# Hybrid encoder trunk, last FFN: second product by Strassen's scheme, with sums of weights made by accumulating DMAs

## The chip, the cores and the metric

The kernel runs on one core of one Trainium2 chip. The time is that of one execution on the device in microseconds (us); lower is better. Where several runs are named, their median is meant. TensorE is PE (its weight loads PEld), VectorE DVE, ScalarE ACT, GpSimd POOL, SyncE SP.

## The reference, cut to what matters

A trunk of two layers on 512 tokens of width 1024. Each layer has a token mixer and then a SwiGLU FFN, each of them between two RMS norms, with shift, scale and gate from a conditioning vector. The change touches the second layer's FFN, the last thing computed, and its tail:

```python
def swiglu_ffn(h, w_in, w_out):
    gate, up = jnp.split(h @ w_in, 2, axis=-1)
    return (jax.nn.silu(gate) * up) @ w_out        # (512 x 2816) @ (2816 x 1024)

def reference(...):
    ...
        h = rmsnorm(x, norm_g[i, 2]) * (1.0 + scale) + shift
        y = swiglu_ffn(h, f_w_in[i], f_w_out[i])
        x = x + gate * rmsnorm(y, norm_g[i, 3])
    return x
```

Everything is float32. The kernel makes a float32 product on TensorE from two parts of each operand: a high part, rounded to the format `fp32r`, and a low part, the difference from it. Three matmuls stand for one: high x high, high x low, low x high.

## The kernel before

The last FFN is the call `ffn(3, 1, ...)` at the kernel's end. Its first product (`w1`, 1024 x 5632) gives gate and up, 22 blocks of 128 rows each, with tokens along the free dimension (512 in one PSUM bank). The first six blocks (`lead_ps`) are begun in the boundary behind the mixer and finished by `rest`; the other 38 are made by `in_chunk`, 24 matmuls of 128x512 each. `load_w` (L209 to L222) loads two blocks of weights (1 MB) over SP's queue into a `wst` buffer and has `split_w` (L203, L204) make the two parts in a `whl` buffer: ACT casts the high part, DVE subtracts. For each f, `ff_act` (L964 to L968) takes silu of the gate on ACT, multiplies by up on DVE, casts the high part on ACT and subtracts on DVE. So the 22 activation tiles `ff0` to `ff21` (128 rows of the hidden dimension x 512 tokens, two parts) lie ready before the second product.

The second product is made by `out_begin`, `out_finish` and `Boundary` (L346 on). For each column half of `w2` (512 columns) and each k of 22, `mm_tiles` (L378 to L380) multiplies the four token groups of 128 by the two parts of the weights: 22 x 4 x 2 x 3 matmuls. Token groups are output rows here, and the eight results (two halves, four groups) fill all eight PSUM banks. Weights of 4 x 128 rows x 512 columns come by `load_wo` (L233) into `wst` buffers and are split into `whl` tiles of two row blocks. At the end each token group in turn gets its last matmuls (`m0`, `m1a`, `m1b`), the sum of squares on ACT (`sq`, L427), the product with the gate and norm row on DVE (`yg_`, L431), the root (`rt1`, L441), the reciprocal (`rc1`, L444) and the new x (`x`, L448), which SP's queue stores; the last half of the last group is cut in two (`x_end`, L456 and L457).

Buffers: `wst` has 2, `whl` 4, `t2` (temporaries of 128x512) 4; the eight `h` tiles hold the FFN's input. The order of PE, ACT and DVE is written out by hand in the boundaries and at the end (`manual_schedule`), and in the first layer's FFN; in this `ffn` a scheduler sets it, except for PE in `rest`. Instructions of an engine run in order, and so do the DMAs of a queue: one that waits holds up what is behind it.

Of the kernel before, what the change touches and what calls it, by code (L numbers as in the profile page):

```python
# [8 lines left out]
F32 = mybir.dt.float32  # L9
F32R = mybir.dt.float32r  # L10
AF = mybir.ActivationFunctionType
# [5 lines left out]
P = 128  # L17
T = 512
D = 1024
KD = D // P  # L20
DFF = 2816
NF = DFF // P
# [13 lines left out]
def trunk_kernel(  # L36
# [26 lines left out]
    def t2(name):  # L63
        return tmp.tile([P, T], F32, tag="t2", name=name, bufs=4)
# [52 lines left out]
    xt = [hp.tile([P, D], F32, name=f"x{t}", tag=f"x{t}") for t in range(4)]  # L117
# [88 lines left out]
    def load_w(srcs, nk=KD, k0=0, later=None):  # L206


        st = wst_p.tile([P, 8, 256], F32, tag="wst", name="wst")  # L209
        o = 0  # L210
        for m, c0, n in srcs:
            dma(st[:, :nk, o:o + n], m[k0 * P:(k0 + nk) * P, c0:c0 + n].rearrange("(k p) f -> p k f", p=P))
            o += n
        res = []
        for b in range(o // P):
            w = whl_p.tile([P, 2, 8, P], F32R, tag="whl", name="whl")
            sw = st[:, :nk, b * P:(b + 1) * P]
            if later is None:
                split_w(sw, w, nk)
            else:  # L220
                later.append((lambda sw=sw, w=w: act.copy(w[:, 0, :nk, :], sw),  # L221
                              lambda sw=sw, w=w: dve.tensor_tensor(w[:, 1, :nk, :], sw,  # L222
                                                                   w[:, 0, :nk, :].bitcast(F32), SUB)))
            res.append(w)
        return res
# [63 lines left out]
    def in_chunk(w, h):  # L289
        pst = mm_ps("ip")  # L290
        mm_chunk(pst, w, h)
        return pst
# [9 lines left out]
    def small(n):  # L302
        return tmp.tile([P, n], F32, tag=f"ss{n}", name="ss", bufs=8)

    gate_d = dram.tile([4, KD, P], F32, name="gate_d")
# [11 lines left out]
    def make_gg(s, gg):  # L317

        gg = gg()
        dma(gg, gate_d[s].rearrange("j p -> (j p)").partition_broadcast(P))  # L320
        return gg
# [232 lines left out]
    def out_finish(parts, *ready):  # L554
        first, second, finish = parts
        for part in (first, second):
            for ops in part:
                for op in ops:
                    op()
        return finish(*ready)  # L560
# [9 lines left out]
    with ExitStack() as ph:  # L570
# [10 lines left out]
        def act_tile(name):  # L581
            return actp.tile([P, 2, T], F32R, tag="a", name=name)
# [12 lines left out]
        h = [hp.tile([P, 2, T], F32R, tag=f"h{j}", name=f"h{j}") for j in range(4)]  # L595
# [20 lines left out]
        lead = {}  # L616
# [66 lines left out]
        with tc.manual_schedule(engines={PE_ENGINE, mybir.EngineType.SP, mybir.EngineType.Activation,  # L683
# [41 lines left out]
            s2, b1 = small(2), small(1)  # L725
# [18 lines left out]
            lead_ps = [None] * 6  # L744
# [101 lines left out]
            splits, ws, acts, us, ggs = [], [], [], {}, []  # L846
            t0 = {}

            def load_pair(p):
                jp, kind = 2 + p // 3 * 2, (1, 2, 0)[p % 3]  # L850
                ws.extend(load_w([(w_in0, kind * D + jp * P, 256)], later=splits))
# [31 lines left out]
            for p in range(2):  # L883
# [12 lines left out]
            tiles = []  # L896
            parts = out_begin(0, w_out0, lambda k: acts[k], KD, ggs, xn_tile, "aux", None,
                              ffn_after(0), ada_tile)
            for k in range(18):
                i, jp = k % 6, 2 + k // 6 * 2  # L900
# [45 lines left out]
            lead, todo = ffn_lead(0, tile4), [[] for _ in range(5)]  # L946
# [7 lines left out]
            begun = out_finish(parts, tail, ws0)  # L954


        def ffn(s, i, begun, act_tile, gg_tile, xn_tile, lead, after):
            w1, w2 = f_w_in[i], f_w_out[i]
            acts = []
            h, lead_ps, rest, more = begun  # L960

            def ff_act(psg, psu, f):
                g = t2("g")
                act.activation(g, psg, AF.Silu)  # L964
                dve.tensor_mul(g, psu, g)
                a = act_tile(f"ff{f}")
                act.copy(a[:, 0, :], g)
                dve.tensor_tensor(a[:, 1, :], g, a[:, 0, :].bitcast(F32), SUB)  # L968
                acts.append(a)

            for f in range(0, NF, 2):
                if f == 0:
                    with tc.manual_schedule(engines={PE_ENGINE}):
                        for i in (0, 2, 1, 3, 4, 5):
                            rest(i)
                    pss = lead_ps[:4]
                elif f == 2:
                    pss = lead_ps[4:] + [in_chunk(w, h) for w in more]
                else:
                    pss = [in_chunk(w, h) for w in load_w([(w1, f * P, 256)]) + load_w([(w1, DFF + f * P, 256)])]  # L980
                for b in range(2):
                    ff_act(pss[b], pss[2 + b], f + b)
                if f == 18:
                    gg = make_gg(s, gg_tile)
            return out_finish(out_begin(s, w2, lambda k: acts[k], NF, [gg], xn_tile, "aux", lead, after))

        def ssd_lead():
            return (load_lead([(wm_in, 6144, NH), (wm_in, DIN, P)], tile4)
                    + load_lead([(wm_in, DIN + P, P), (wm_in, 2 * DIN, P)], tile4)
# [3 lines left out]
        h, lead_ps, rest, more = begun  # L993
        acts, ws, splits, gates, lows, todo, ggs = [], list(more), [(), ()], {}, [], [], []
# [4 lines left out]
        def gate(f, pst):  # L999
            gates[f] = t2("g")  # L1000
            act.activation(gates[f], pst, AF.Silu)

        def up(f, pst):
            g, a = gates[f], act_tile(f"ff{f}")
            dve.tensor_mul(g, pst, g)
            act.copy(a[:, 0, :], g)
            acts.append(a)
            lows.append(lambda: dve.tensor_tensor(a[:, 1, :], g, a[:, 0, :].bitcast(F32), SUB))
# [20 lines left out]
        with tc.manual_schedule(engines={PE_ENGINE, mybir.EngineType.SP, mybir.EngineType.Activation,  # L1029
# [14 lines left out]
            tiles = []  # L1044
            for k in range(2 * NF - 6):
# [8 lines left out]
                q, j = divmod(k - 3, 4)  # L1054
# [19 lines left out]
        begun = out_finish(parts)  # L1074
        h, lead_ps, rest, wz1 = begun
# [4 lines left out]
    with ExitStack() as ph:  # L1080
# [99 lines left out]
        class Group:  # L1180
# [169 lines left out]
            def root(self):  # L1350
                self.rg = t2("rg")
                act.activation(self.rg, self.ssg, AF.Sqrt, bias=eps_t, scale=1.0 / 256)
# [201 lines left out]
        with tc.manual_schedule(engines={PE_ENGINE}):  # L1554
# [3 lines left out]
            gg2.append(make_gg(2, lambda: tile4b([P, D], F32, "gg")))  # L1558
            begun = out_finish(parts)

    with ExitStack() as ph:
        actp3 = ph.enter_context(tc.tile_pool(name="actp3", bufs=22, reuse_waits="tile"))
        ffn(3, 1, begun, lambda n: actp3.tile([P, 2, T], F32R, tag="a", name=n),
            lambda: actp3.tile([P, D], F32, tag="gg", name="gg", bufs=1), None, None, None)


# [27 lines left out]
```

## Time and profile before

| | |
|---|---|
| median of 3 runs | 1366.4 us (1366.18 to 1366.81) |
| the profiled execution: its time | 1366.3 us |
| its span (first to last instruction in the trace) | 1364.5 us |
| last FFN, first product by `in_chunk` | 1031.8 to 1238.5 us |
| last FFN, second product | 1238.5 to 1358.4 us |
| from the last matmul to the end of the span | 1358.5 to 1364.5 us |
| mean granted clock of TensorE | 0.999 |

All times inside the profile count from the start of the span. A row of a group names the line, the engine, the operation, the tiles (output <- inputs), their shapes and the count; behind the bar the busy time in us and the mean of one in ns, then the idle time of the engine just ahead of them and what ended it. In a timeline or a chain the first number is the start in us, the second the length. The busy time of one instruction overlaps that of the next by a little, so the step from one start to the next is shorter than the length of one.

### The profile page before, as it was taken

What the parts mean: (1) busy time and instruction counts of PE and PEld (TensorE: products, weight loads), DVE (VectorE), ACT (ScalarE), POOL (GpSimd) and SP (SyncE); (2) the same over time, 40 slices, a digit from 0 to 9 for tenths busy, and PEclk for the clock granted to TensorE, in tenths of its full rate; (3) what the DMA queues carried; (4) which work ended last, traced back from release to release, by engine and by line L of the source; (5) the groups of instructions that cost most, each with busy time, mean ns of one, the idle gap of its engine ahead of it and who ended that gap; (6) DMA issues with size and microseconds to landing.
All of it is one profiled execution on the core that took longest, in us unless ns stands there. A gap on an engine that the chain in (4) does not pass through costs nothing.

```text
span 1364.5 us, 17280 instructions
## 1 busy us (share of the span) xinstructions
PE 1353.1 (99%) x6975; PEld 1139.0 (83%) x6975; DVE 849.5 (62%) x1344; ACT 539.6 (40%) x826; POOL 11.6 (1%) x23
## 2 busy tenths in 40 slices
PE   8999999999999999999999999999999999999998
PEld 6788889888888888898888888888898888888886
DVE  5578766787776322759988898897672333333224
ACT  5333355222322222745655545464572232222112
POOL 0000000000000000000000000000000000000000
PEclk9999999999999999999999999999999999999999
DMA  9767750777776232325343433313502332222221
GB/s 311 233 182 241 230 198 17 251 227 246 223 241 215 97 111 90 108 62 160 108 140 110 138 97 105 131 60 119 184 27 83 107 105 98 93 93 93 93 93 62
DMA packets 154212, 190.35 MB, mean 140 GB/s; under 512 B 5892, under 2 KB 111252, under 8 KB 153108
## 3 DMA queue, kind: packets, MB, share of 16 engines
q1 hardware_dynamic: 149984, 176.34, 40.8%
q10 hardware_dynamic: 4148, 12.90, 3.1%
q8 instruction: 55, 0.90, 0.3%
q14 instruction: 25, 0.20, 0.0%
HBM read 186.98 MB, written 2.24 MB: 139 GB/s over the span
## 4 chain that ended last, share of the span: by engine, by line
PE 97%; SPq 2%; DMA 1%; ACT 0%; DVE 0%; issue 0%; DVEq 0%; ACTq 0%
PE ip L276 18%; PE ip L278 18%; PE ip L277 18%; PE y L378 9%; PE y L380 9%; PE y L379 9%; PE li L276 3%; PE li L278 3%; PE li L277 3%; PE li L756 1%; PE yd L1313 1%; SPq L611 1%; PE yo L1307 1%; PE xtr L494 1%; DMA ada_st<-in_ada_w_dram 1%; PE cb L1252 1%
## 5 line engine op out<-in xcount | busy, mean ns | idle before, releaser
L276 PE MATMUL ip<-h,whl 128*128 128x512 f32 x1096 | 430.8, 393 | 0.2 <-DVE cv L863 0.2
L278 PE MATMUL ip<-h,whl 128*128 128x512 f32 x1096 | 426.8, 389 | 0.0
L277 PE MATMUL ip<-h,whl 128*128 128x512 f32 x1096 | 426.5, 389 | 0.0
L276 PEld LDWEIGHTS ip<-h,whl 128*128 128x128 f32 x1096 | 205.8, 188 | 43.9 <-issue 1.8
L278 PEld LDWEIGHTS ip<-h,whl 128*128 128x128 f32 x1096 | 205.7, 188 | 43.3
L277 PEld LDWEIGHTS ip<-h,whl 128*128 128x128 f32 x1096 | 205.8, 188 | 41.8
L204 DVE TENSOR_TENSOR whlo<-wsto,whlo 128x1024 fp32r<-128x1024 f32 x63 | 76.9, 1224 | 162.8 <-ACT whlo L203 162.7
L222 DVE TENSOR_TENSOR whl<-wst,whl 128x1024 fp32r<-128x1024 f32 x96 | 116.7, 1221 | 59.8 <-ACT whl L221 59.6
L378 PE MATMUL y<-whlo,ff 128*128 128x512 f32 x352 | 137.1, 390 | 0.0
L380 PE MATMUL y<-whlo,ff 128*128 128x512 f32 x352 | 136.9, 389 | 0.0
L379 PE MATMUL y<-whlo,ff 128*128 128x512 f32 x352 | 136.9, 389 | 0.0
L203 ACT CAST whlo<-wsto 128x1024 fp32r<-128x1024 f32 x63 | 65.8, 1051 | 162.6 <-PE y L380 149.5
L204 DVE TENSOR_TENSOR whl<-wst,whl 128x1024 fp32r<-128x1024 f32 (+1 forms) x77 | 72.7, 973 | 87.4 <-ACT whl L203 87.4
L124 DVE SCALAR_TENSOR_TENSOR ada_acc<-ada_st,csil,ada_acc 128x512 f32<-128x512 f32 x140 | 105.0, 750 | 4.0 <-DMA ada_st<-in_ada_w_dram 0.5
L221 ACT CAST whl<-wst 128x1024 fp32r<-128x1024 f32 x96 | 99.8, 1041 | 4.1 <-DMA wst<-in_m_w_in_dram 2.4
L203 ACT CAST whl<-wst 128x1024 fp32r<-128x1024 f32 (+1 forms) x77 | 62.6, 846 | 91.1 <-PE ip L278 39.8
L276 PE MATMUL li<-h,whl 128*128 128x256 f32 x288 | 83.2, 289 | 0.0
L278 PE MATMUL li<-h,whl 128*128 128x256 f32 x288 | 81.6, 283 | 0.0
L277 PE MATMUL li<-h,whl 128*128 128x256 f32 x288 | 81.5, 283 | 0.0
L380 PEld LDWEIGHTS y<-whlo,ff 128*128 128x128 f32 x352 | 66.1, 188 | 13.8
L379 PEld LDWEIGHTS y<-whlo,ff 128*128 128x128 f32 x352 | 66.1, 188 | 13.7
L378 PEld LDWEIGHTS y<-whlo,ff 128*128 128x128 f32 x352 | 66.1, 188 | 13.5
(235 smaller groups left out, 1643.9 us busy)
## 6 DMA issues: line engine op xcount, KB each, us to landing
ada_st<-in_ada_w_dram SPq DMA_DIRECT2D x96, 512.0 KB, 5.1
wst<-in_f_w_in_dram SPq DMA_DIRECT2D x44, 1024.0 KB, 5.2
wsto<-in_f_w_out_dram SPq DMA_DIRECT2D x20, 1024.0 KB, 5.0
wst<-in_m_w_in_dram SPq DMA_DIRECT2D x14, 1024.0 KB, 5.4
wst<-in_m_w_in_dram SPq DMA_DIRECT2D x20, 512.0 KB, 5.3
wst<-in_a_w_in_dram SPq DMA_DIRECT2D x9, 1024.0 KB, 6.0
csb<-cs_d ACTq DMA_DIRECT2D x8, 1024.0 KB, 5.1
wsto<-in_m_w_out_dram SPq DMA_DIRECT2D x7, 1024.0 KB, 6.4
```

What stands on the lines that cost most here:

```text
L124: dve.scalar_tensor_tensor(acc, w, csil[:, k:k + 1], acc, MUL, ADD)
L203: act.copy(dst[:, 0, :nk, :], src)
L204: dve.tensor_tensor(dst[:, 1, :nk, :], src, dst[:, 0, :nk, :].bitcast(F32), SUB)
L221: later.append((lambda sw=sw, w=w: act.copy(w[:, 0, :nk, :], sw), lambda sw=sw, w=w: dve.tensor_tensor(w[:, 1, :nk, :], sw, w[:, 0, :nk, : ...
L222: lambda sw=sw, w=w: dve.tensor_tensor(w[:, 1, :nk, :], sw, w[:, 0, :nk, :].bitcast(F32), SUB)))
L276: pe.matmul(dst, w_at(w, 0, kk), a[:, 0, sl], start=start, stop=False)
L277: pe.matmul(dst, w_at(w, 0, kk), a[:, 1, sl], start=False, stop=False)
L278: pe.matmul(dst, w_at(w, 1, kk), a[:, 0, sl], start=False, stop=stop)
L378: pe.matmul(pst, a[:, 0, tk], wt[:, 0, kk, :], start=k == 0, stop=False)
L379: pe.matmul(pst, a[:, 0, tk], wt[:, 1, kk, :], start=False, stop=False)
L380: pe.matmul(pst, a[:, 1, tk], wt[:, 0, kk, :], start=False, stop=k == K - 1)
L494: pe.transpose(pt[:, j * 256 + t * P:j * 256 + (t + 1) * P], self.xn[2 * hi + t][p // 2][:, c:c + P], ident)
```

## The change

The second product of the last FFN is cut 2 x 2 x 2: the 512 tokens into halves of 256, the 1024 columns into halves of 512, and the 22 row blocks of the hidden dimension into two sets of 11, the even and the odd ones. A pair of neighbouring row blocks, p = 0 to 10, gives one block to each set, so `b11`, `b12`, `b21`, `b22` of a pair are four quarters of 128 x 512 (first digit: row set, second: column half), and `a11`, `a12`, `a21`, `a22` of 128 x 256 (first digit: token half, second: row set). Strassen's scheme in Winograd's form makes seven products of halves. Products 1 to 7 are, in this order, b11 with a11; b21 with a12; b22 with a12; b22 with a11; b12 with s1; b11 with a21; b21 with a22, where every name but the first few stands for what lies in that place by then: sums of quarters.

* Sums of activations are made by DVE in place (`s13`, `a_prep`); the unsplit activations lie in `raw`, and `s1` in `s1t`.
* Sums of weights are made by DMAs from GpSimd's queue with `accum_op=ADD`: T1 (b12 += b11), T3 (b11, reloaded with the raw b12 by SP's queue, += b22), T2 (b22 += b12), T4 (b21 += b22). Units are two double pairs, (0,1) and (2,3), and seven single ones; one DMA each per unit and sum.
* The weights of the second product are loaded whole: units 0 to 2 into `w2t` tiles during the first product, 3 and 4 into `wst` buffers at its end, 5 to 8 into the `h` tiles once the first product is over.
* The 77 steps (product, p) are taken in pairs, "tiles" n = 0 to 38. For each, `w_prep(n)` makes the two parts of the weights in a `whl` buffer (4 of them) and `a_prep(n)` those of the activations in an `ao` buffer (3), ACT casting and DVE subtracting; `products` issues the matmuls, 12 for a tile. After the matmuls of tile n come `behind(n)` (sums of products out of the banks A, B, C, D, epilogue work, and the DMAs for T2 to T4), then `w_prep(n + 4)` and `a_prep(n + 3)`. The order of all engines is written by hand from the start of this FFN.
* Results: 11 = A after product 1, plus B; 12 = C - A after product 4, + D; 22 = D - A after product 6; 21 = A after product 7. The first token half is finished while products 6 and 7 run; the last three tiles are issued for token group 2 first, then for group 3.

The first product keeps its matmuls. The second has 7 x 11 x 2 x 3.

```diff
-        def ffn(s, i, begun, act_tile, gg_tile, xn_tile, lead, after):
-            ...
-            return out_finish(out_begin(s, w2, lambda k: acts[k], NF, [gg], xn_tile, "aux", lead, after))
...
+    PRODUCTS = (("A", "b11", "a11"), ("B", "b21", "a12"), ("C", "b22", "a12"), ("A", "b22", "a11"),
+                ("D", "b12", "s1"), ("A", "b11", "a21"), ("A", "b21", "a22"))
...
+        def s13(p, n):
+            dve.tensor_tensor(a_("s1", p, n), a_("a21", p, n), a_("a22", p, n), SUB)
+            dve.tensor_tensor(a_("a21", p, n), a_("a11", p, n), a_("a21", p, n), SUB)
+
+        def up(f, pst):
+            dve.tensor_mul(raw[:, f, :], pst, gates[f])
+            if f % 4 == 3:
+                s13(f // 2 - 1, 2)
+            elif f == NF - 1:
+                s13(f // 2, 1)
+
+        even = list(range(NP))
+        odd = [4, 0, 1, 2, 3] + list(range(5, NP))
+        steps = [(i, p) for i in range(7) for p in (odd if i % 2 else even)]
+        NT = (len(steps) + 1) // 2
...
+        def a_prep(n):
+            ...
+            for sl, (i, p), m in todo:
+                srca = a_(PRODUCTS[i][2], p, m)
+                act.copy(a[:, 0, sl, :], srca)
+                dve.tensor_tensor(a[:, 1, sl, :], srca, a[:, 0, sl, :].bitcast(F32), SUB)
+            for _, (i, p), m in todo:
+                if i == 0:
+                    dve.tensor_tensor(a_("a11", p, m), a_("s1", p, m), a_("a11", p, m), SUB)
+                elif i == 1:
+                    dve.tensor_add(a_("a12", p, m), a_("a12", p, m), a_("a11", p, m))
...
+            def add_(dst, src):
+                pool.dma_start(dst, src, accum_op=ADD)
...
+            def t3(i):
+                u = units[i]
+                for q, p in enumerate(u):
+                    dma(b_(i, "b11", q), w2_rows(p)[:, 0, 0, T:])
+                add_(b_(i, "b11"), b_(i, "b22"))
...
+            up(NF - 1, tiles[-1])
+            ht = [hp.tile([P, 1, D], F32, tag=f"h{j}", name=f"w2h{j}") for j in range(KD)]
+            ...
+            for n in (2, 3):
+                w_prep(n)
+            a_prep(2)
+            for i in range(3, len(units)):
+                t1(i)
...
+            def behind(n):
+                if n == 2:
+                    for i in range(len(units)):
+                        t3(i)
+                for i, u in enumerate(units):
+                    if n - 8 == u[-1] // 2:
+                        t2_(i)
+                if n == 18:
+                    for i in range(len(units)):
+                        t4(i)
+                for t in range(2):
+                    ...
+                    elif n == 27:
+                        dve.tensor_add(got["12", t], got["12", t], bank["D"][t])
+                        got["22", t] = spare[f"c22_{t}"]
+                        act.copy(got["22", t], bank["D"][t])
+                    elif n == 28:
+                        square(t, 0, got["11", t])
+                        square(t, 1, got["12", t])
+                        mean(t)
+                    elif n == 29:
+                        root(t)
+                        for hf, c in enumerate(("11", "12")):
+                            gated(got[c, t], hf, got[c, t])
+                    elif n == 30:
+                        for hf, c in enumerate(("11", "12")):
+                            x_new(t, hf, got[c, t])
+                    elif n == 32:
+                        dve.tensor_tensor(got["22", t], got["22", t], bank["A"][t], SUB)
+                    ...
+
+            for n in range(NT - 3):
+                products([n])
+                behind(n)
+                ...
+                if n + 4 < NT:
+                    w_prep(n + 4)
+                if n + 3 < NT:
+                    a_prep(n + 3)
+            products(range(NT - 3, NT))
```

More of the change, by code (lines that the diff above doesn't have):

```diff
@@ L954, in trunk_kernel @@
             begun = out_finish(parts, tail, ws0)
-        def ffn(s, i, begun, act_tile, gg_tile, xn_tile, lead, after):
[L958 to L984, printed above, removed]
-            return out_finish(out_begin(s, w2, lambda k: acts[k], NF, [gg], xn_tile, "aux", lead, after))
         def ssd_lead():
```

161 lines of the change are left out of this document (158 added, 3 removed).

## The prediction

> **What bounds the kernel now.** First the busy shares of the whole span, then the two stages of the last FFN by windows (its first product from 1031.8, its second from 1238.5 us), then the groups of instructions of the second, then the end.
>
> ```profile
> PE 1353.1 (99%) x6975; PEld 1139.0 (83%) x6975; DVE 849.5 (62%) x1344; ACT 539.6 (40%) x826; POOL 11.6 (1%) x23
> ...
> 1238.50:1358.40 119.90, 119.88 (x529) 98.91 (x527) 33.92 (x41) 27.42 (x38) 0.00 (x0) 1.00 0.23 82
> 1031.80:1238.50 206.70, 206.70 (x914) 171.17 (x913) 70.38 (x76) 58.09 (x75) 0.00 (x0) 1.00 0.28 92
> ...
> L378 PE MATMUL y<-whlo,ff 128*128 128x512 f32 x176 | 68.5, 389 | 0.0
> L204 DVE TENSOR_TENSOR whlo<-wsto,whlo 128x1024 fp32r<-128x1024 f32 x19 | 23.3, 1225 | 75.7 <-ACT whlo L203 75.7
> L203 ACT CAST whlo<-wsto 128x1024 fp32r<-128x1024 f32 x19 | 20.0, 1054 | 82.2 <-PE y L380 74.5 <-PE ip L278 3.9 <-issue 3.9
> L431 DVE TENSOR_TENSOR yg<-y,gg 128x512 f32<-128x512 f32 x8 | 5.5, 686 | 4.6 <-ACT junk L427 4.6
> L448 DVE SCALAR_TENSOR_TENSOR x<-yg,ss,x 128x512 f32<-128x512 f32 x7 | 5.0, 748 | 0.1
> L427 ACT ACTIVATE junk<-y 128x512 f32<-128x512 f32 x8 | 4.8, 596 | 13.8 <-PE y L380 13.8
> L427 ACT ACTIVATION_READ_ACCUMULATOR junk<-y 128x1 f32 x8 | 1.6, 194 | 0.0
> L441 ACT ACT_TABLE_LOAD x1 | 1.3, 1283 | 0.0
> L441 ACT ACTIVATE ss<-ss 128x1 f32<-128x1 f32 x4 | 1.2, 294 | 0.1
> L444 DVE RECIPROCAL ss<-ss 128x1 f32<-128x1 f32 x4 | 0.6, 156 | 0.9 <-ACT ss L441 0.9
> ```
>
> A window's row gives its length, then the busy time of PE, PEld, DVE, ACT and POOL, the granted clock, the DMA share and GB/s. In both stages PE is busy all the time at clock 1.00 and L378 has no idle time before it: matmuls alone set the pace. The second product has 528 of them (22 row blocks x 4 token groups x 2 column halves x 3 parts; the row of L378 has a third) in 119.9 us: 0.227 us each. DVE works 33.9 of these 119.9 us and ACT 27.4; L204 waits 75.7 us for the casts, these for PE to give buffers back. So a matmul that goes is worth 0.227 us as long as DVE and ACT keep up.
>
> **The matmuls that go: -15.0 us.** Seven products of 11 row blocks x 2 token groups x 3 parts are 462 matmuls, of the same shape. 66 x 0.227 = 15.0.
>
> **The preparation.** Now PE consumes tiles of two steps: 12 matmuls, 2.72 us. For each, ACT casts and DVE subtracts one weight pair (128x1024, or twice 128x512 where the blocks lie in separate tiles) and one activation pair (128x512), which the kernel before did once for all uses and before this stage. What DVE and ACT need for an operation that follows another, from pairs and fours:
>
> ```profile
> 1017.14 4.63 DVE L204 TENSOR_TENSOR whl<-wst,whl 128x1024 fp32r<-128x1024 f32 x4 [0.53 <-ACT whl L203]
> ...
> 1030.96 1.29 DVE L968 TENSOR_TENSOR ff<-g,ff 128x512 fp32r<-128x512 f32 x2 [2.53 <-ACT ff L967]
> ...
> 1348.70 1.41 DVE L448 SCALAR_TENSOR_TENSOR x<-yg,ss,x 128x512 f32<-128x512 f32 x2
> ...
> 1030.32 1.13 ACT L967 CAST ff<-g 128x512 fp32r<-128x512 f32 x2
> ...
> L512 DVE TENSOR_TENSOR h<-u,h 128x256 fp32r<-128x256 f32 x16 | 6.5, 422 | 5.6 <-ACT h L508 5.5
> L967 ACT CAST ff<-g 128x512 fp32r<-128x512 f32 x22 | 13.5, 617 | 0.0
> ```
>
> Four in 4.63 us with 1.225 for the last: 1.135 each; by the same step 0.605 for a 128x512 subtraction, 0.66 for the scalar form of L448, and 0.51 for a 128x512 cast. An operation on the result of the one before needs its full 0.69.
>
> *Start of the stage.* I count from the first Strassen matmul. The last gate product must leave PSUM first, and DVE then has in its order: that product 0.69, two 128x256 sums 0.84, the splits of tiles 2 and 3's weights 4 x 0.605, tile 2's activations 0.69: with 0.25 to begin, ready at 4.9, wanted at 2 x 2.72 = 5.44. Cost 0.
>
> *First two products* (tiles 2 to 11). To the splits comes one sum of activations in place, 0.69: at most 2 x 0.605 + 0.605 + 0.69 = 2.50 of 2.72 us per tile. DVE gains 0.2 per tile. Cost 0; were every DVE operation 15% longer (2.88), ten tiles would be 1.6 late, less the 0.5 in hand.
>
> *The end of the first two token groups* (`behind(27)` to `behind(32)`). Here the order written by hand puts epilogue work between the splits. From the end of tile 27's matmuls: DVE adds bank D twice (to 1.3), ACT copies D out (2 x 0.5) and casts tile 31's weights and tile 30's activations (to 3.4), DVE follows to 4.3. Then ACT squares four times, 0.598 + 0.194 each, to 6.6, and only then casts tile 32's weights and tile 31's activations: DVE has those at 9.1, PE wanted tile 31 at 8.2 (its last part 0.45 later): **0.5 late**. Table load 1.28 and roots: 9.9. DVE: two reciprocals and four gate products (to 12.4), then 1.135 + 0.605 for tiles 33 and 32: 14.2, wanted at 11.9: **2.3 late**. DVE: four L448 forms, 2.64, tiles 34 and 33, 1.74, tiles 35 and 34, 1.81, and only behind these the subtraction from bank A (0.69): 20.95. Product 7 accumulates into that bank, so tile 33's first matmul waits for it; wanted at 16.4: **4.5 late**. Sum 7.4: of these 20.95 us DVE works 16.4 and waits for ACT most of the rest, while PE has 13.6 us of work. Bounds: 0, since the rows show DVE off the path at every epilogue of before; above, the 7.4 with all of it 15% longer, 10.
>
> *The last end.* PE finishes tokens 256 to 383, then 15 matmuls (3.4 us) for the last group; the first's epilogue takes 0.25 + 0.79 + 0.69 + 0.16 + 1.41 = 3.3 on DVE under them. Behind the last matmul stands the same chain as now:
>
> ```profile
> 1358.15 0.24 PE y L380
> ...
> 1359.19 0.69 DVE yg L431
> ...
> 1359.99 0.75 DVE x L448
> 1360.74 0.40 DVEq L1589
> 1361.13 0.40 DVE x L456
> ```
>
> Cost 0.
>
> **The clock.** A gap of 4.5 us is new to this stage. What the trace shows of one:
>
> ```profile
> 1358.00:1359.00 1.00, 0.38 (x2) 0.00 (x0) 0.00 (x0) 0.53 (x2) 0.00 (x0) 1.00 0.92 346
> 1360.00:1361.00 1.00, 0.00 (x0) 0.00 (x0) 1.00 (x2) 0.00 (x0) 0.00 (x0) 0.86 0.00 0
> 1362.00:1363.00 1.00, 0.00 (x0) 0.00 (x0) 0.00 (x0) 0.00 (x0) 0.00 (x0) 0.50 1.01 349
> ```
>
> The last matmul ends at 1358.5; 0.86 over the slice 1360 to 1361 puts the fall to 0.50 at 1360.7, 2.2 us later. So the clock can fall within the gap ahead of tile 33. Half the clock costs 0.227 us for each matmul; for how long isn't shown. Ends: 0, and 1.8 if it lasts as long as the trace's own stretch at 0.50 (3.7 us). I take the middle, 0.9. The Trainium skill, "TensorE: Matmul & The Clock Gate" (Part 1), says that an idle window of about 3.4 us halves the clock and a busy one of that length restores it; by that alone a gap of 4.5 us costs up to 1.7 us, and the sum would be 0.8 higher. The trace's 2.2 us is shorter than the page's window.
>
> **The adds in the DMA queues.** T1 to T4 are 36 DMAs that GpSimd issues, each adding 256 KB (two blocks of them 512 KB), in one order: T1, T3, T2, T4, each waiting at the queue's head for its operands; whatever is behind it waits too. SP reloads 2.75 MB for T3. No row shows an accumulating DMA. The nearest:
>
> ```profile
> wsto<-in_f_w_out_dram SPq DMA_DIRECT2D x4, 512.0 KB, 3.7
> out_dram<-x SPq DMA_DIRECT2D x7, 256.0 KB, 2.0
> ...
> 6.00:8.00 2.00, 1.21 (x12) 1.02 (x11) 1.08 (x3) 1.74 (x6) 0.00 (x0) 1.00 0.96 378
> ```
>
> At 378 GB/s 256 KB take 0.7 us of the engines. Call D what one 256 KB add occupies of the queue. T1 matters to nobody for long, T3 only from tile 27, T4 from tile 33. The tight one is T2 of row-block pair 4, which product 4 uses first: DVE frees its operand at 29.4, ACT wants the sum at the end of tile 12, 35.4, and PE feels it from 39.5 on (tile 15's activations stand behind it on ACT). Sixteen adds of 256 KB (eleven of T3, five of T2) must be through by then, from about 10 on (16 loads into the h tiles and the first reloads, 0.7 each): stall = 16 D - 29.5, so D up to 1.8 is hidden. Two reads and one write at the shown rate are 1.4 at least if nothing overlaps within an add; without any overlap between adds D is the 2.0 of a whole 256 KB store, or the 3.7 of the 512 KB load. Adds in a queue overlap as the loads do, so I take 1.4: cost 0, ends 0 and 44 (below). The Trainium skill, "DMA: Bandwidth & Descriptors" (Anatomy of one DMA), gives a GpSimd-issued DMA 2.0 us fixed plus bytes over 436 GB/s: 2.6 for 256 KB. Were that paid one after the other, the stall would be 12 us at tile 16 alone; no run here shows it.
>
> **Sum.** 1364.5 - 15.0 + 7.4 + 0.9 = 1357.8 of span; the median of the runs is 1.9 above the span (1366.4; the profiled execution itself 1366.3): **1359.7**.
>
> **Rivals.** (1) *The adds are slow.* From the point where T2 of pair 4 misses 39.5, PE waits 16 D - 29.5, and the other six pairs then come every D instead of the 1.36 that PE takes for one: 22 D - 37.7 in all. It makes the kernel slower than before from D = 2.0. At D = 2.6 it costs 19.5: 1379; at 3.7, 44: 1403. For it: nothing in the trace bounds an add, POOL is shown busy 11.6 us only, and the limit is as low as one plain store. Against: queued loads overlap, and the stage before moves only 82 GB/s. (2) *The epilogue fits*: ACT and DVE slip past each other so that bank A is free in time. 1366.4 - 15.0 = 1351.4. Against it: three in-order queues with the waits above. (3) *DVE is slowed by something in the new stage*, 15% and more: 3 us by the first and last terms, growing with each tile; 1363 to 1367.
>
> **How the numbers follow.** The forecast has 0.47 (own range 1355 to 1363), rival 1 0.32, rival 2 0.14, rival 3 0.07. 0.2% is 2.7 us, about what a measurement of this kernel can tell from no change. Faster: 0.47 + 0.14 + 0.03 of rival 3 = 0.64. Within: 0.04 of rival 3 and 0.03 of rival 1 with D at 2.0: 0.07. Slower: 0.29. The range goes from below rival 2, 1350.5, to rival 1 at D = 2.6, 1380; about half of rival 1 lies above it.
>
> **What would show it.** PE idle, by DVE, at bank A's first matmul of product 7 (about 4.5 us) and 2 to 3 us a tile before, and none in the first 70 us of the stage: right. A wait of casts or of PE for GpSimd's queue near tile 16: rival 1. No idle at bank A: rival 2. Subtractions clearly longer than 1.225 and 0.69: rival 3. A second product (first to last Strassen matmul) shorter than 106 or longer than 119.9 us would make the prediction wrong in size or in sign.

## The result, and the profile after

The changed kernel takes 1377.6 us (median of 4 runs, 1376.8 to 1379.0), the kernel before 1366.5 us in the same session: a ratio of 1.0083 (95% interval 1.0065 to 1.010). It is slower by 11 us; 1359.7, faster by 7, was forecast.

First the busy times of the whole span (page, part 1), then windows of the new stage, from its first matmul at 1238.8 us to the last at 1371. A row gives the length, the busy time of PE, PEld, DVE, ACT and POOL, the granted clock, the DMA share and GB/s.

```profile
PE 1345.5 (98%) x6909; PEld 1130.4 (82%) x6909; DVE 898.0 (65%) x1437; ACT 570.4 (41%) x893; POOL 46.1 (3%) x59
...
1238.80:1371.00 132.20, 111.93 (x463) 90.00 (x461) 88.74 (x142) 68.54 (x123) 29.30 (x31) 0.90 0.60 134
...
1270.00:1280.00 10.00, 9.77 (x44) 7.75 (x42) 4.35 (x7) 2.88 (x6) 5.21 (x6) 1.00 0.96 162
1280.00:1290.00 10.00, 0.00 (x0) 0.00 (x0) 0.00 (x0) 0.00 (x0) 3.38 (x3) 0.66 0.67 115
1290.00:1300.00 10.00, 5.41 (x13) 4.13 (x14) 4.93 (x7) 4.16 (x7) 5.23 (x6) 0.50 0.98 166
1300.00:1310.00 10.00, 10.00 (x45) 8.24 (x44) 6.13 (x10) 7.61 (x13) 3.36 (x3) 0.99 0.63 108
```

The 66 matmuls are gone (6975 before, 6909 now), yet the second product is longer: 132.2 us instead of 119.9. From 1280 to 1290 PE, DVE and ACT do nothing; only POOL and the DMA engines work. The clock falls to 0.50 in that gap, at 1283.2, and is back at 1300.3. PE's timeline in that stage, with its three gaps in brackets (start, length, count; the idle time ahead and what ended it):

```profile
1268.73 11.04 PE L1650 MATMUL cC<-whlo,ao 128*128 128x512 f32 x48
1294.59 6.33 PE L1650 MATMUL cC<-whlo,ao 128*128 128x512 f32 x15 [14.82 <-ACT ao L1628]
...
1302.14 14.44 PE L1650 MATMUL cA<-whlo,ao 128*128 128x512 f32 x63
...
1332.06 12.55 PE L1650 MATMUL cA<-whlo,ao 128*128 128x512 f32 x53
1346.63 3.47 PE L1650 MATMUL cA<-whlo,ao 128*128 128x512 f32 x10 [2.02 <-DVE ao L1629]
1353.52 8.87 PE L1650 MATMUL cA<-whlo,ao 128*128 128x512 f32 x28 [3.41 <-DVE w2h L1779]
```

Sixty-three matmuls without disturbance take 14.44 us, 63 x 0.2267 + 0.16. The gaps sum to 20.25 us. By the same rule the 15 matmuls behind the first gap should take 3.56 and take 6.33, the 10 behind the second 2.43 and take 3.47, the 28 behind the third 6.51 and take 8.87: 6.2 us more, at half the clock. Gaps and half clock are 26.5 us. The row of 53 takes 0.4 us more than the rule's 12.17: PE waits a little within it, at tile 31.

The chain of work that ended last, in order of time (start, length, who), tells where the first gap is from; rows of GpSimd's timeline stand for T1 (1254.09), T3 (1258.22 and 1266.38) and T2 (1281.61 and 1286.99), and the waits view names what held ACT:

```profile
1241.07 5.47 DMA w2h<-in_f_w_out_dram
1248.05 6.03 issue
...
1267.13 1.41 POOL w2t L1657
1268.54 3.40 issue
...
1287.72 5.66 DMA w2t<-w2t
1294.59 6.33 PE cC L1650 x15
```

```profile
1254.09 0.86 POOL L1657 DMA_DIRECT2D w2h<-w2h  x1 [4.86 <-PE cA L1650]
1258.22 1.22 POOL L1657 DMA_DIRECT2D w2t<-w2t  x1 [3.27 <-DVE whlo L1616]
1266.38 2.16 POOL L1657 DMA_DIRECT2D w2t<-w2t  x2 [6.94 <-DVE whlo L1616]
...
1281.61 1.22 POOL L1657 DMA_DIRECT2D w2t<-w2t  x1 [2.27 <-issue]
1286.99 2.17 POOL L1657 DMA_DIRECT2D w2t<-w2t  x2 [4.16 <-issue]
...
ACT whlo L1615 <- DMA w2t<-w2t: 18.4, 1, 18.4
```

The path runs over GpSimd's queue from the loads of the h tiles to an add that lands at 1293.4: T2 of row-block pair 4, the third T2 (the second add in the row at 1286.99). ACT stands 18.4 us at the cast of that pair's weights, behind it the cast of tile 15's activations, and so PE (14.8). T3 starts at 1258.22, 19.4 us into the stage, and from there to the landing 16 blocks of 256 KB take 35.2 us: 2.2 us each.

What the operations of the stage cost, by groups (those of DVE and ACT answer to L204, L968 and L203 of before), and the queue of the adds (part 3 of the page):

```profile
L1616 DVE TENSOR_TENSOR whlo<-w2t,whlo 128x1024 fp32r<-128x1024 f32 x12 | 14.7, 1221 | 4.5 <-ACT whlo L1615 4.4
L1629 DVE TENSOR_TENSOR ao<-raw,ao 128x512 fp32r<-128x512 f32 x28 | 19.2, 684 | 0.0
L1615 ACT CAST whlo<-w2t 128x1024 fp32r<-128x1024 f32 x12 | 12.6, 1050 | 8.6 <-PE cA L1650 4.3 <-PE cB L1650 2.2 <-PE cD L1650 2.1
...
q0 software_dynamic: 6208, 11.54, 4.9%
```

DVE and ACT are as fast as before (1221 to 1225 ns, 684 to 686). The 36 adds are 44 blocks of 256 KB (11.54 MB); 4.9% of 1377.2 us of all 16 DMA engines is 1.53 us for a block.

### The profile page after: what moved, and what is told of

Read it like the earlier page. It is cut to its first block, busy times and chain, and to the rows that moved or that the text cites. A ratio compares the mean times of both kernels' runs of the same rounds, so it can differ in the third digit from the quotient of the medians.

```text
span 1377.2 us, 17423 instructions
## 1 busy us (share of the span) xinstructions
PE 1345.5 (98%) x6909; PEld 1130.4 (82%) x6909; DVE 898.0 (65%) x1437; ACT 570.4 (41%) x893; POOL 46.1 (3%) x59
## 3 DMA queue, kind: packets, MB, share of 16 engines
q0 software_dynamic: 6208, 11.54, 4.9%
## 4 chain that ended last, share of the span: by engine, by line
PE 91%; issue 3%; SPq 2%; DMA 1%; DVE 1%; ACT 1%; POOL 1%; DVEq 0%; POOLq 0%; ACTq 0%
PE ip L276 18%; PE ip L278 18%; PE ip L277 18%; PE y L378 6%; PE y L380 6%; PE y L379 6%; PE li L276 3%; PE li L278 3%; PE li L277 3%; PE cA L1650 2%; PE li L756 1%; PE yd L1283 1%; PE cD L1650 1%; SPq L611 1%; PE yo L1277 1%
## 5 line engine op out<-in xcount | busy, mean ns | idle before, releaser
L222 DVE TENSOR_TENSOR whl<-wst,whl 128x1024 fp32r<-128x1024 f32 x132 | 160.7, 1221 | 133.5 <-ACT whl L221 133.4
L221 ACT CAST whl<-wst 128x1024 fp32r<-128x1024 f32 x132 | 136.6, 1042 | 32.1 <-PE ip L278 23.7
L204 DVE TENSOR_TENSOR whlo<-wsto,whlo 128x1024 fp32r<-128x1024 f32 x41 | 49.9, 1224 | 78.4 <-ACT whlo L203 78.2
L203 ACT CAST whlo<-wsto 128x1024 fp32r<-128x1024 f32 x41 | 42.6, 1049 | 76.3 <-PE y L380 74.8
L1650 PE MATMUL cA<-whlo,ao 128*128 128x512 f32 x264 | 64.9, 405 | 5.4 <-DVE w2h L1779 3.4
L378 PE MATMUL y<-whlo,ff 128*128 128x512 f32 x176 | 68.6, 390 | 0.0
L380 PE MATMUL y<-whlo,ff 128*128 128x512 f32 x176 | 68.5, 389 | 0.0
L379 PE MATMUL y<-whlo,ff 128*128 128x512 f32 x176 | 68.5, 389 | 0.0
L1650 PEld LDWEIGHTS cA<-whlo,ao 128*128 128x128 f32 x264 | 51.3, 196 | 18.1 <-issue 4.1
L1142 DVE SCALAR_TENSOR_TENSOR cu<-ip,cols,cu 128x511 f32<-128x511 f32 (+2 forms) x84 | 62.8, 748 | 3.9 <-ACT cu L1139 1.4
L1585 ACT ACTIVATE g<-ip 128x512 f32<-128x512 f32 x18 | 10.8, 598 | 121.9 <-PE ip L278 121.9
L276 PEld LDWEIGHTS li<-h,whl 128*128 128x128 f32 x288 | 55.3, 192 | 0.0
```

Of the source, the lines that this page charges most:

```text
L204: dve.tensor_tensor(dst[:, 1, :nk, :], src, dst[:, 0, :nk, :].bitcast(F32), SUB)
L222: lambda sw=sw, w=w: dve.tensor_tensor(w[:, 1, :nk, :], sw, w[:, 0, :nk, :].bitcast(F32), SUB)))
L276: pe.matmul(dst, w_at(w, 0, kk), a[:, 0, sl], start=start, stop=False)
L378: pe.matmul(pst, a[:, 0, tk], wt[:, 0, kk, :], start=k == 0, stop=False)
L379: pe.matmul(pst, a[:, 0, tk], wt[:, 1, kk, :], start=False, stop=False)
L380: pe.matmul(pst, a[:, 1, tk], wt[:, 0, kk, :], start=False, stop=k == K - 1)
```

## The experiments

The theory after this: two separate losses, the late T2 of pair 4 (with the half clock behind it) and the crowded end of the first two token groups (with its own). Rivals: the losses have one cause, or the stage is slow in itself (its matmuls, its splits). All times are medians in us; the kernel before took 1366.3 to 1366.5 beside each of them. A row that begins with dots builds on the one above it, the row of copies and that of some T3 left out do not.

| kernel | time (range) | ratio to before (95% interval) |
|---|---|---|
| changed kernel | 1377.6 (1376.8 to 1379.0) | 1.0083 (1.0065 to 1.010) |
| no adds | 1360.6 (1360.1 to 1361.0) | 0.9957 (0.9943 to 0.9972) |
| spread end | 1368.5 (1367.4 to 1370.2) | 1.0016 (1.0006 to 1.0025) |
| no adds, spread end | 1351.4 (1351.2 to 1352.0) | 0.9889 (0.9875 to 0.9902) |
| blocks of 256 KB | 1371.4 (1370.3 to 1371.5) | 1.0035 (1.0022 to 1.0048) |
| ... T3 right ahead of its T2 | 1380.8 (1380.1 to 1381.0) | 1.0104 (1.0088 to 1.0121) |
| ... wanted blocks first | 1367.4 (1364.5 to 1368.0) | 1.0001 (0.9992 to 1.001) |
| ... and spread end | 1356.7 (1355.9 to 1357.3) | 0.9928 (0.9915 to 0.9942) |
| ... and T3 earlier | 1356.2 (1355.8 to 1357.0) | 0.9927 (0.9911 to 0.9944) |
| plain copies | 1361.3 (one run) | |
| some T3 left out, spread end | 1356.1 (1355.9 to 1356.4) | 0.9925 (0.991 to 0.994) |
| five T2 blocks on DVE, spread end | 1352.6 (1352.1 to 1353.1) | 0.990 (0.9885 to 0.9914) |
| ... each a tile later | 1351.3 (1351.3 to 1351.4) | 0.9889 (0.9872 to 0.9905) |

### Each loss alone, and both

```diff
             def add_(dst, src):
-                pool.dma_start(dst, src, accum_op=ADD)
+                pass
```

> Leaves out: the 36 accumulating DMAs (the sums of weights are not made; the reloads for T3 stay). Everything else is as in the changed kernel. Theory A (GpSimd's queue holds PE up ahead of bank C, 14.8 us, and the half clock after it costs 2.9 us more): both go, 1377.6 - 17.7 = 1360, and the gaps of 2.0 and 3.4 us near the end with their slow clock stay as they are. Rival C (the preparation on DVE and ACT is what is late, and the wait for the DMA only hides it): another wait shows at the same place, 1370 or more.

Measured 1360.6. The gap of 14.8 us is gone; the two at the end are still there:

```profile
PE cA L1650 <- DVE w2h L1779: 2.7, 1, 2.7
PE cA L1650 <- DVE ao L1629: 2.0, 1, 2.0
```

The other loss: squares, gate products and new x of the first two token groups, which stood together behind tiles 28 to 30, are handed out over tiles 22 to 35, and the splits of the two tiles after it stand behind the subtraction from bank A.

```diff
-                    elif n == 28:
-                        square(t, 0, got["11", t])
-                        square(t, 1, got["12", t])
-                        mean(t)
...
+                    if n == 22 + t:
+                        square(t, 0, got["11", t])
+                    if n == 24 + t:
+                        gated(got["11", t], 0, got["11", t])
...
+                    if n == 28 + t:
+                        square(t, 1, got["12", t])
+                        mean(t)
...
-                if n + 4 < NT:
-                    w_prep(n + 4)
-                if n + 3 < NT:
-                    a_prep(n + 3)
+                for m in {31: (), 32: (31, 32)}.get(n, (n,)):
+                    if m + 4 < NT:
+                        w_prep(m + 4)
+                    if m + 3 < NT:
+                        a_prep(m + 3)
```

> Adds as in the changed kernel. Only the epilogue of the first two token groups is spread out: squares and gate products of half 11 at tiles 22 to 25, the table load for the root at 25, the rest one piece per tile from 28 to 35, and the splits of tiles 35 and 34 behind the subtraction from bank A. Theory (the gaps of 2.0 and 3.4 us are the bunched epilogue on ACT and DVE, and the half clock behind them costs about 4 us): all of that goes, 1377.6 - 9.4 = 1368. Rival (the gaps are a lack of DVE time as a whole in that stretch): gaps move but stay, gain below 3 us. The wait of 14.8 us stays in both.

Measured 1368.5. Both gaps at the end are gone, and the last 129 matmuls of bank A run at full clock; the first gap stays. PE's timeline:

```profile
1293.74 6.35 PE L1650 MATMUL cC<-whlo,ao 128*128 128x512 f32 x15 [14.22 <-ACT ao L1628]
...
1331.25 29.42 PE L1650 MATMUL cA<-whlo,ao 128*128 128x512 f32 x129
```

Both edits at once:

> Adds left out (so the sums of weights are missing from the output) and the end of the first two token groups spread out. Theory (the two losses, late adds and the gap at the end, are separate and add): taking out each alone gave -17.0 us (1377.6 to 1360.6) and -9.1 us (1377.6 to 1368.5), so both give 1377.6 - 17.0 - 9.1 = 1351.5 us, which is also 1366.4 less the 15.0 us of 66 matmuls; no gap of PE and no half clock in the stage. Rival (the losses overlap, or the clock of the one hangs on the other): 1354 to 1360 us.

Measured 1351.4. The two losses add up, to within 0.1 us: 17.0 and 9.1 alone, 26.2 together. Nothing else slows the stage: 1366.5 - 1351.4 is 15.1 us, the 66 matmuls.

### Why an add costs 2.2 us

Double blocks cut into two DMAs of 256 KB:

```diff
-                pool.dma_start(dst, src, accum_op=ADD)
+                for q in range(dst.shape[1]):
+                    pool.dma_start(dst[:, q, :], src[:, q, :], accum_op=ADD)
```

> Each add of a double unit is issued as two adds of 256 KB instead of one of 512 KB; same bytes, same order. Theory A1 (little room for descriptors in GpSimd's queue: a double add only goes when the one before it has drained, so the 16 adds ahead of pair 4's T2 take 2.2 us each instead of the 1.5 us that their packets take): no gaps between bursts of packets, T2 of pair 4 lands some 8 to 10 us sooner, PE waits 5 to 7 us instead of 14.8, time 1366 to 1369. Rival A2 (the DMA engines' own rate, shared with loads, sets the 2.2 us): wait and time as in the changed kernel, 1377, or later, since there are 8 more DMAs.

Measured 1371.4, between the two. PE's first gap is 7.7 instead of 14.8 us. And with plain copies in place of adds:

```diff
-                pool.dma_start(dst, src, accum_op=ADD)
+                pool.dma_start(dst, src)
```

> Every add is a plain copy from the same queue, same order and sizes as in the changed kernel (so the sums are not formed). Theory (an add reads and writes its target as well, and that fills the DMA engines: 1.53 us of all 16 per 256 KB): a copy takes the 0.8 to 0.9 us that the loads of the h tiles show (311 GB/s at a share of 1.02), T2 of pair 4 lands some 10 us earlier, PE's gap of 14.8 us falls to 0 to 5 us, time 1362 to 1367 us. Rival (what sets the pace is how many descriptors of GpSimd's queue are in flight, whatever they do): the gap stays at 13 to 15 us, 1376 to 1378 us.

Measured 1361.3 (one run), and neither PE nor ACT waits for the queue. Windows of 20 us in which the queue of adds is at work, for the changed kernel, for blocks of 256 KB and for copies; the last two numbers of a row are the DMA share and GB/s:

```profile
1282.00:1302.00 20.00, 7.41 (x21) 5.74 (x22) 6.16 (x10) 6.05 (x11) 8.22 (x9) 0.57 0.83 141
```

```profile
1282.00:1302.00 20.00, 15.09 (x54) 12.10 (x55) 10.65 (x17) 11.35 (x20) 11.51 (x14) 0.74 1.03 175
```

```profile
1264.00:1284.00 20.00, 20.00 (x90) 16.57 (x89) 15.60 (x24) 12.44 (x22) 11.64 (x21) 1.00 0.86 319
...
q0 software_dynamic: 3392, 11.54, 2.3%
```

A block copied takes 2.3% of 1359.5 us over 44, 0.71 us of the engines; the same block added takes 1.53, and the 44 take 6208 packets instead of 3392. So the add is what is dear, not the queue as such. With blocks of 256 KB the engines are full (1.03; a share of 1 or a little over is full) and a block goes through every 1.4 to 1.6 us. The double blocks leave them idle in between (0.83): in the changed kernel's rows above GpSimd stands 2.27 and 4.16 us ahead of double blocks with nothing named but "issue".

The landing times in the traces tell what it waits for, and it is what theory A1 said. In blocks of 256 KB each add from 1253 us on is issued 0.31 us after an earlier one has landed, with two more still under way: there are never more than three. A double block counts as two, and goes only when at most one block is under way. The view of transfers has the double block issued at 1281.61 (its size, then us from issue to landing):

```profile
w2t<-w2t POOLq DMA_DIRECT2D x1, 512.0 KB, 5.0
```

The next one, at 1286.99, is issued 0.34 us behind that landing, with nothing under way: between two double blocks the engines run empty. Of the copies up to six are under way at once. Why it is three for adds isn't shown.

### Where in the queue the wanted block stands

In blocks of 256 KB from here on. T3 of units 3 and up put right ahead of T2 of the same unit, so that T2 of pair 4 comes sooner:

```diff
                 if n == 2:
-                    for i in range(len(units)):
+                    for i in range(3):
                         t3(i)
                 for i, u in enumerate(units):
                     if n - 8 == u[-1] // 2:
+                        if i >= 3:
+                            t3(i)
                         t2_(i)
```

> As the single adds, and T3 of units 3 to 8 is issued just ahead of T2 of the same unit instead of ahead of all T2, so ten adds instead of sixteen stand ahead of and include pair 4's T2. Theory A (what is queued ahead in GpSimd's one queue makes it late): no wait at bank C or under 2 us; time 1360 as without any adds. Rival A2 (rate): ten adds at 2.2 us still from 1258 on land at 1280, PE waits 2 to 3 us and later units are late as well, 1364 or more.

A miss: 1380.8, slower than the changed kernel. GpSimd's timeline:

```profile
1289.94 1.78 POOL L1658 DMA_DIRECT2D w2h<-w2h  x2 [3.72 <-DVE ao L1629]
1295.41 1.75 POOL L1658 DMA_DIRECT2D w2h<-w2h  x2 [3.69 <-DVE whlo L1616]
1301.10 1.78 POOL L1658 DMA_DIRECT2D w2h<-w2h  x2 [3.94 <-DVE ao L1629]
```

T2 overwrites the b22 that T3 reads, so each T2 waits at the queue's head until its T3 has landed, with the next unit's T3 behind it: 5.5 us for two blocks. (The brackets name DVE; by the landing times each T2 goes 0.6 to 0.7 us after its T3 has landed, with nothing under way.) PE's wait went from pair 4 to the later pairs, three gaps of 15.0 us together. The next order keeps some blocks between a T3 and its T2:

```diff
                 if n == 2:
-                    for i in range(len(units)):
-                        t3(i)
-                for i, u in enumerate(units):
-                    if n - 8 == u[-1] // 2:
-                        t2_(i)
+                    for i in range(0, len(units)):
+                        reload(i)
+                    for i in range(0, 5):
+                        t3(i)
+                if n == 10:
+                    for i in (2, 0, 1, 3):
+                        t2_(i)
+                if n == 11:
+                    t2_(4)
+                    for i in range(5, 9):
+                        t3(i)
+                    t2_(5)
...
```

> All 36 blocks added, in blocks of 256 KB, in another order: T3 of units 0 to 4 first, then T2 of unit 2 (pair 4, the first that ACT wants), T2 of units 0, 1, 3, 4, then T3 of the rest between, each T3 some blocks ahead of its T2. Theory (the stall is the place of T2 of pair 4 in the queue, 16 blocks of 1.4 to 1.6 us behind the first T3): it now stands 8th, lands about 1272 instead of 1284.7 us in the trace of singles, PE waits for no add, and the time is that without adds, 1360.6 us; the gaps of 2.0 and 2.7 us at the end stay. Rival (the 16 DMA engines are full, so the order only moves the wait to the last pairs): a gap of 3 to 7 us at pairs 7 to 10, 1364 to 1369 us.

1367.4: the rival's time and place. Nothing waits at pair 4; a gap of 3.7 us is left where ACT stands at the casts of pairs 7 and 8, and the ends' 2.0 and 4.3. With the spread end:

> The same order and the spread end together. Theory: 1351.5 us, 14.9 us less than before, PE without a gap in the stage. Rival (as for the order alone: a wait at pairs 7 to 10): 1355 to 1360 us.

1356.7, the rival again: one gap, 3.0 us, and the half clock behind it. Would T3 help if it began earlier?

```diff
             for c, r in ((0, 0), (0, 1), (1, 0), (1, 1)):
+                if (c, r) == (1, 0):
+                    w_prep(2)
+                    for i in range(3):
+                        reload(i)
...
+            for i in (3, 4):
+                t1(i)
+            for i in range(3):
+                t3(i)
+            for i in range(5, len(units)):
+                t1(i)
```

> Spread end; the reloads and T3 of units 0 to 2 go ahead of the second half of the loads of the h tiles and of T1 of units 5 to 8, and all T3 ahead of all T2. Theory (from 1239 to the last T2 the 16 DMA engines are full with 27 blocks of 0.84 us and 28 adds of about 1.4 us, so an earlier start of the one puts off the other): about the time of the other order with the spread end, 1354 to 1358 us, with a gap of PE of 2 to 4 us. Rival (the late start of T3, 16.5 us into the stage, is the cause): no gap, 1351.4 us.

1356.2, the same. T3 of unit 0 now goes at 1245.9 instead of 1255.7 us, but a gap of 2.0 us is back at pair 4 (all T3 stand ahead of T2 here). The engines are full all the way, so in this order one block's gain is another's loss; the DMA share is the number before the last:

```profile
1240.00:1260.00 20.00, 20.00 (x90) 16.56 (x89) 19.79 (x34) 12.59 (x23) 5.28 (x6) 1.00 1.03 306
1260.00:1270.00 10.00, 10.00 (x46) 8.29 (x45) 9.31 (x15) 6.48 (x10) 4.43 (x6) 1.00 1.08 221
1270.00:1280.00 10.00, 9.16 (x41) 7.25 (x39) 3.73 (x6) 2.29 (x4) 6.00 (x7) 1.00 1.01 189
```

### Some of the adds on DVE

If the engines are full, blocks have to leave them. T2 of units 0 to 2, five blocks, goes to DVE; all T3 stand ahead of the other T2.

```diff
+                if n in (10, 11):
+                    for i in ((2,), (0, 1))[n - 10]:
+                        for q in range(len(units[i])):
+                            dve.tensor_add(b_(i, "b22", q), b_(i, "b22", q), b_(i, "b12", q))
+                for i in range(3, len(units)):
+                    if n == max(11, 8 + units[i][0] // 2):
+                        t2_(i)
```

> All sums formed, spread end, blocks of 256 KB, all T3 ahead of T2; the five T2 blocks of units 0 to 2 are added by DVE (5 x 0.6 us) instead of by DMAs, which takes 5 x 1.5 = 7.5 us out of the full DMA engines ahead of the last pairs. Theory: the last T2 lands about 1286 to 1288 us, before ACT wants it (about 1290); no gap of PE, 1351.4 us, 15 us less than before. Rival (DVE, at 7 of 10 us in these tiles, becomes late in turn): a gap named for DVE of 1 to 4 us, 1353 to 1358 us.

1352.6, 1% faster than before. The rival has a point: one gap of 1.15 us, by DVE, whose first add stood 1.96 us until its T3 had landed. (DVE's timeline, then PE's.)

```profile
1270.26 0.69 DVE L1754 TENSOR_TENSOR w2t<-w2t 128x512 f32<-128x512 f32 x1 [1.96 <-DMA w2t<-w2t]
...
1278.22 5.98 PE L1650 MATMUL cC<-whlo,ao 128*128 128x512 f32 x25 [1.15 <-DVE ao L1629]
```

```diff
-                if n in (10, 11):
-                    for i in ((2,), (0, 1))[n - 10]:
-                        for q in range(len(units[i])):
-                            dve.tensor_add(b_(i, "b22", q), b_(i, "b22", q), b_(i, "b12", q))
+                for i, q in {11: ((2, 0),), 12: ((0, 0), (0, 1)), 13: ((1, 0),), 14: ((1, 1),)}.get(n, ()):
+                    dve.tensor_add(b_(i, "b22", q), b_(i, "b22", q), b_(i, "b12", q))
```

> As the kernel with five T2 blocks on DVE, but each of these adds stands one tile or more later and at most two behind one tile (unit 2 behind tile 11, unit 0 behind 12, unit 1 behind 13 and 14). There DVE stood 1.96 us at its first add, until T3 of unit 2 had landed, and PE then waited 1.15 us for DVE, without a drop of the clock. Theory: the add finds T3 landed, the gap goes, 1351.4 us, that is 1.2 us less than the 1352.6 of the kernel before it. Rival (DVE has no room for 5 adds of 0.6 us at any place in these tiles): the gap moves and stays at 1 us or grows, 1352.5 us or more.

1351.3, with no gap of PE in the stage: 15.1 us less than before, with all sums formed. Windows, where the first gap had been:

```profile
1270.00:1280.00 10.00, 10.00 (x46) 8.29 (x45) 9.65 (x17) 5.24 (x10) 6.42 (x8) 1.00 0.97 164
1280.00:1290.00 10.00, 10.00 (x46) 8.29 (x45) 7.57 (x12) 7.61 (x13) 5.39 (x7) 1.00 1.03 176
```

The DMA engines are as full as ever, but what they still have to do is wanted later.

### What a gap does to the clock

```diff
             def t3(i):
...
-                add_(b_(i, "b11"), b_(i, "b22"))
+                if i not in (3, 4, 5, 6):
+                    add_(b_(i, "b11"), b_(i, "b22"))
```

> Spread end, adds in blocks of 256 KB in the changed kernel's order, the adds T3 of units 3 to 6 left out (four sums missing from the output). With all T3 in this order PE waited 7.7 us; four blocks of 1.5 us less leave one gap of about 1.7 us, and no other gap in the stage. Theory (any gap of about 2 us drops the clock, which then costs 1.5 to 3 us more): 1351.4 + 1.7 + 2 = 1355 us, with matmuls at twice 227 ns after the gap. Rival (the clock only drops after a gap of over some 3 us, and the drop after the gap of 2.0 us in the other traces came from the gap behind it): 1353.1 us, no matmul above 227 ns.

1356.1, the theory with a little more: one gap of 2.1 us, and behind it 15 matmuls take 5.64 us instead of 3.56. PE's timeline and four windows:

```profile
1281.67 5.64 PE L1650 MATMUL cC<-whlo,ao 128*128 128x512 f32 x15 [2.09 <-ACT ao L1628]
...
1282.00:1283.00 1.00, 0.92 (x4) 0.48 (x3) 0.83 (x2) 1.00 (x3) 0.83 (x1) 1.00 1.01 170
1283.00:1284.00 1.00, 1.00 (x4) 0.74 (x4) 1.00 (x2) 1.00 (x2) 0.29 (x2) 0.50 1.11 188
1285.00:1286.00 1.00, 1.00 (x3) 0.77 (x3) 1.00 (x2) 0.00 (x0) 0.77 (x1) 0.50 1.01 170
1286.00:1287.00 1.00, 1.00 (x5) 0.78 (x4) 0.23 (x1) 0.34 (x1) 0.50 (x2) 0.79 1.07 182
```

The gap ends at 1281.67; the clock falls at 1283.0, when PE has been at work again for 1.3 us, and stays at 0.50 for 3.4 us (0.79 is 0.42 us of the last slice).

Not every gap of about 2 us does this. With plain copies there is one of 2.02 us ahead of 1328.32, and behind it ten matmuls take 2.60 us. The clock stays at 1.00 until it falls at 1334.5, within the next gap, of 4.28 us (PE's timeline, then windows of PE alone):

```profile
1328.32 2.60 PE L1650 MATMUL cA<-whlo,ao 128*128 128x512 f32 x10 [2.02 <-DVE ao L1629]
...
1324.00:1331.00 7.00, 4.90 (x20) 1.00 0.19 68
1334.50:1341.00 6.50, 5.80 (x14) 0.50 0.00 0
```

The last section says what sets the two apart.

## Why the prediction was wrong, point by point

**The step that failed: "The adds in the DMA queues", cost 0.** It cost 14.8 us of waiting and, with the half clock behind it, 17.0 us of time (1377.6 to 1360.6 without the adds). The step asked the right question: T2 of pair 4 was called the tight one, tile 15's activations on ACT the place where PE feels it, the stall 16 D - 29.5. Both numbers put into it were off. D, taken at 1.4, was 2.2: at the front of it the engines' own time for an add, 1.53, somewhat above the 1.4 that stood for two reads and one write (1.4 is two passes of 0.7; three, with nothing overlapping as the step has it, would be 2.1 and by its formula a stall of 4.1 us). Then there are the pauses around the double blocks, which were not thought of. And the chain of T3 began not "from about 10 on" but at 19.4 us: the T1 ahead of it wait for the loads of the h tiles (until 1246.58) and then for one another, three under way at a time, and the loads, T3's own reloads and the adds share engines that are full (share 1.02 from 1240 to 1260, quoted below). At 2.2 the formula gives 5.7 us, the start adds 9.4: 15.1, and 14.8 was measured. (Both numbers are read off the same trace, so this bears out the 39.5 at which PE feels a late T2, no more.) That is rival 1, in its place. The adds did overlap: blocks of 256 KB pass every 1.4 to 1.6 us. The 2.6 us for one, the estimate from the Trainium skill ("DMA: Bandwidth & Descriptors", Anatomy of one DMA), are not paid one after the other here. What rival 1 added for the other six pairs did not come: while PE stood, the queue went on.

**The clock, 0.9 us: mis-sized.** It measured 6.2 us: 2.8 behind the gap of the adds and 3.4 behind the two at the end. The step took the middle between nothing and 3.7 us at half the clock, a stretch that had ended only because the trace does, and put the fall into the gap ahead of tile 33. In fact it came earlier, at 1348.1, behind the gap of only 2.0 us, and the clock was back at 1358.3: 10.2 us, with some 15 matmuls to pay for it. By the rule of the Trainium skill that was set beside it, "TensorE: Matmul & The Clock Gate" (Part 1), it takes an idle window of about 3.4 us, so a gap of 2.0 would leave the clock alone. The trace differs.

**The end of the first two token groups, 7.4 us: right in kind, somewhat high.** The gaps came where they were put, in tile 32 (2.0, forecast 2.3) and at bank A (3.4, forecast 4.5); at tile 31 there was 0.4 (forecast 0.5), within the row of 53 matmuls. 5.8 us in all, and the spread end took 9.1 us off the time, since it took their half clock (3.4) along.

**The matmuls that go, -15.0 us: right**, to 0.1 us, by the kernel without adds and with the spread end, and by the best one.

**Start of the stage, first two products, last end, 0 each: right.** Behind the last matmul the span goes on for 6.2 us, before for 6.0. PE has no gap in the first 41 us though DVE works 19.76 of the 20 us from 1240:

```profile
1240.00:1260.00 20.00, 20.00 (x90) 16.57 (x89) 19.76 (x34) 13.21 (x24) 4.73 (x5) 1.00 1.02 311
```

Rival 3 (DVE slower) falls with the rows of L1616 and L1629. Rival 2's time, 1351.4, needed both losses gone. With the terms as measured, 1364.5 - 15.0 + 14.8 + 5.8 + 6.2 = 1376.3 of span, of 1377.2. The range (1350.5 to 1380) held the time; the chances had slower at 0.29.

## What to carry to other kernels

A sum handed to DMAs isn't free because its queue is idle: price an add at twice a copy of its size, add it to every other transfer of the same stretch, and compare with the time until the first result is wanted. Where the DMA engines were full all the way, no order tried here made up for it; a few blocks on an engine with room (here five adds of 0.6 us on DVE) can be worth more. And an order written by hand needs its blocks put by when they are wanted, with several others between an add and one that must wait for it.

A gap of PE costs more than its length: here 1 to 3 us more for each that the clock followed, and it did not follow each. Taking away each suspected loss alone and then both told within three kernels that they add and that nothing else was lost.

## What the hardware showed that was not expected

* An add by DMA costs the engines 2.2 times a copy (1.53 against 0.71 us per 256 KB) and GpSimd 0.86 us to issue. No more than three adds of 256 KB were under way at a time. The Trainium skill, "Collectives: The Full Stack" (Part 3, The bandwidth ceiling), says that a reduce reads two sources and so gets half the rate of a copy, there of a collective. These runs agree, roughly, for an accumulating DMA within SBUF.
* For the clock it counted where a gap lay, not its length alone. In each trace the changes of the clock from 1230 us on lie whole multiples of 3.41 us apart: the stretches at 0.50 before the last matmul last 3.41 us (with the lone gaps of 2.04, 2.09 and 3.0 us), 6.83, 10.24 (over the two gaps at the end of the changed kernel) or 17.07 (with the gap of 14.8 us, from 1283.2 to 1300.3). Count in steps of 3.41 us from such a change. In all fourteen traces a step in which PE was idle for 1.92 us or more left the clock at half, one with 1.71 us or less did not take it down, and it came back behind the first step with 0.36 us or less (0.66 was too much). So the gap of 2.09 us, which lay within one step (1279.60 to 1283.01), halved the clock. The gap of 2.02 us with plain copies, cut by the end of a step at 1327.71 into 1.41 and 0.61, left it alone, and so did the gap of 1.15 us. How a program could choose the place of a gap isn't shown.
